# Second-half convolution beside the first half's attention, a norm in other PSUM banks, and softmax scaling on GpSimd

## The chip, the cores and the metric

The kernel runs on one core of a Trainium2 chip. A core has five engines that run their own instruction streams and wait for each other by semaphores: TensorE (PE in the profile: matrix products and transposes; PEld is its weight load), VectorE (DVE), ScalarE (ACT), GpSimd (POOL) and SyncE (SP, which here issues most of the loads). Tiles lie in SBUF, and the results of TensorE in PSUM, which is divided into banks of 128 partitions by 512 fp32 values. The metric is the device time of one execution in microseconds (us).

## The reference

One decoder layer on 1024 tokens of width 1024, in fp32. The parts that this change touches are the token mixer's two groups:

```python
proj = x @ w_in + b_in
q, k, v, a, gate = jnp.split(proj, [Q_END, K_END, V_END, A_END], axis=-1)
# attention group: window 128, 8 heads, 2 kv heads, a sink per head
scores = jnp.where(mask, scores + bias[:, :, None], -jnp.inf)
m = jnp.maximum(jnp.max(scores, axis=-1, keepdims=True), sink)
p = jnp.exp(scores - m)
denom = jnp.sum(p, axis=-1, keepdims=True) + jnp.exp(sink - m)
probs = (p / denom).astype(v.dtype)
# convolution group
h = a * jax.nn.sigmoid(gate)
h = causal_depthwise_conv(h, dw_w, dw_b)      # 31 taps, 512 channels
h = layer_norm(h, ln_g, ln_b)
y_conv = jax.nn.silu(h)
y = jnp.concatenate([rms_norm(y_attn, attn_out_gain), rms_norm(y_conv, conv_out_gain)], axis=-1)
mix = y @ w_out + b_out
```

After it come `x = layer_norm(alpha * x + mix)`, an up-projection to 2 x 2816 channels, a convolution of width 3, a SwiGLU gate, a down-projection and a last layer norm.

## The kernel before

**Tiling.** The 1024 tokens are two halves (H = 0 and 1) of 512 tokens, a half four blocks (`TB`) of 128. Activations lie transposed, channels on partitions and 512 tokens along the free axis, so that a projection product is one PSUM tile of 128 x 512. To get fp32 accuracy every operand is split into a high and a low part (`split_part`: the high part by ScalarE, line 232, the low one by GpSimd, line 234), and `mm3` makes a product of 24 matmuls: 8 of high with high (line 266), 8 of high with low (267), 8 of low with high (269). The feed-forward part runs for most channels on both halves together (`joint`, a seven-product scheme, lines 790 to 793), for the first six channel chunks on each half alone.

**Stages of a half.** `glu(H, c)` makes the 128 channels of convolution group c: two products into two PSUM tiles, a sigmoid on ScalarE, and one VectorE operation (line 356) that writes the convolution's input `hconv`. `proj_kv` and `proj_q` make keys, values and queries. `conv(H)` takes the four groups in two pairs (`conv_pair`): 26 (H = 1) or 27 (H = 0) of the 31 taps of a group are VectorE operations that accumulate in a PSUM tile of the C banks (lines 419 and 423; the last writes SBUF), and the remaining taps are a multiplication on ScalarE (409) and an addition on GpSimd (413); line 428 joins them. `conv_norm(H)` is the layer norm over the 512 channels, done with matmuls against ones: the mean (443), the variance (454), a product that spreads the reciprocal deviation (462), and after the swish the mean square for the RMS norm (478). Each of these four has a PSUM tile; VectorE reads them on lines 447, 290, 467 and 290.

`attn(H)` has 16 units, one for each block, kv group and pair of heads, in a software pipeline of 21 steps. `front` makes scores (TensorE, 509), adds the bias and finds the row's maximum (VectorE, 514), takes the exponential with its sum and that of the sink (ScalarE, 519 and 521). With the second pair of a group come the sum of the denominators (525), their reciprocal (526) and the scaling of four tiles of 128 x 256 (529). `mid` transposes (539) and splits (541, 542), `back` multiplies with the values (560 to 562) and reads out (567, 569, 572); `tail` is the mean square of the attention output (579). `out_proj(H)` is the output projection (640 to 652) on top of the residual rows that it loads and scales first (625); `ln1(H)` the layer norm after it, with transposes (277 to 281).

**What sets the order.** The stages are Python generators, and the string `SCRIPT` says in which order their steps are written down: each letter advances one of them by a step. `0`: a GLU group of half 0, `x`: a block of the second half's input, `j`/`k`: kv, `i`/`q`: a product of q, `c`/`C`: the convolution of half 0/1, `n`/`N`: its norm, `a`/`A`: an attention step, `g`: a GLU group of half 1, `o`/`O`: output projection, `l`/`L`: layer norm, `f`: feed-forward of half 0, `s`: sums for `joint`. `c` and `C` ran a convolution to its end at once. From this program order a scheduler, at compile time, places the instructions into the engines' streams, by priority and by its own estimate of the times; an instruction earlier in the program goes first when both are ready. Three orders are held by hand: big products keep their order (`chain`), taps keep theirs (`tap`), and loads keep theirs on SyncE's queue (`load`).

**PSUM.** Five tags share the eight banks: A, S and C have two each, T and Y one. `PT` says which tag a stage's tiles take in turn. In the mixer, the products of `glu1`, `kv1`, `q0` and `q1` and of both output projections take A; scores take S; transposes and attention tails T; attention outputs Y; convolution chains C, and before the change the norm's four tiles took C as well. A tile waits until a bank of its tag is free.

**SBUF.** Places are given by hand (`LANES`). The second half's residual rows (`acc`) lie where the second half's `hconv` and the second norm's temporaries (`LANES_NORM1`) lie.

Of the kernel before, what the change touches and what calls it, by code (L numbers as in the profile page):

```python
# [12 lines left out]
AF = mybir.ActivationFunctionType  # L13
ALU = mybir.AluOpType

P = 128
S = 1024
D = 1024
# [15 lines left out]
LINE = 384  # L34
GROUP = 2
ALONE = 6
SCRIPT = ('0hx00j0hxixxiiiacaaaaaaaaaaaaannnaaagaggqqgaaaqkqoAAAoAAAAAo'
          'ACAoAAllAANAAAANAlAlfNfAOOOfOffLLLLsffffsss')
SKEW = (1, 2, 5)
KOFF = (4, 5)  # L40
# [2 lines left out]
XM = (1, 1)  # L43
PT = {'x0': 'AT', 'x1': 'AS', 'glu0': 'AS', 'glu1': 'A', 'kv0': 'A', 'kv1': 'A', 'q0': 'A', 'q1': 'A', 'v0': 'T', 'v1': 'T',
      'joint': 'ATSACSYC',
      'tail': 'T', 'out0': 'A', 'out1': 'A', 'ln0': 'A', 'ln1': 'A', 'up0': 'AY', 'up1': 'AY', 'down0': 'SCY', 'down1': 'S'}
PS = {'A': 2, 'S': 2, 'T': 1, 'Y': 1, 'C': 2}
UNIT = 512
BASE = 384
# [21 lines left out]
def hybrid_layer_kernel(  # L71
# [7 lines left out]
    nc = tc.nc  # L79
# [22 lines left out]
    def psB(shape=(P, 512), tag="T"):  # L102
        return ps.tile(list(shape), F32, name="ps" + tag, tag=tag, bufs=PS[tag])
# [3 lines left out]
    def psk(key, shape=(P, 512)):  # L107
        tags = PT[key]
        k = ps_turn[key] = ps_turn.get(key, -1) + 1
        return psB(shape, tags[k % len(tags)])  # L110

    def f(ap):
        return ap.bitcast(F32)
# [58 lines left out]
    sink = small[:, 8:16]  # L172
# [151 lines left out]
    def pair(i):  # L324
        return area(2 * i), area(2 * i + 1)
# [109 lines left out]

    def conv_norm(H):
        y = cyt[H]
        mean = psB(tag="C")
        sums = [sbt([P, HALF], "nsum") for _ in range(2)]
        for i in range(2):  # L440
            nc.gpsimd.tensor_tensor(out=sums[i], in0=y[2 * i], in1=y[2 * i + 1], op=ALU.add)
        nc.gpsimd.tensor_tensor(out=sums[0], in0=sums[0], in1=sums[1], op=ALU.add)
        nc.tensor.matmul(out=mean, lhsT=ones, rhs=sums[0], start=True, stop=True)
        var = psB((P, 4), "C")
        sqs = []
        for c in range(4):
            nc.vector.tensor_tensor(out=y[c], in0=y[c], in1=mean, op=ALU.subtract)
            sq = sbt([P, HALF], "nsq")
            nc.scalar.square(out=sq, in_=y[c])
            sqs.append(sq)  # L450
        yield
        for t in range(TB):
            for c in range(4):
                nc.tensor.matmul(out=var[:, t:t + 1], lhsT=sqs[c][:, t * P:(t + 1) * P], rhs=ones[:, 0:1],
                                 start=c == 0, stop=c == 3)
        rstd = ring("crstd", 4, 2)
        rsqrt_eps(rstd, var, 4, "nrv")
        dg = sbt([P, TB, P], "nz")
        for t in range(TB):
            nc.vector.tensor_scalar(out=dg[:, t, :], in0=ident, scalar1=rstd[:, t:t + 1], scalar2=None, op0=ALU.mult)  # L460
        rb = psB(tag="C")
        nc.tensor.matmul(out=rb, lhsT=ones1, rhs=dg, start=True, stop=True)
        yield
        yh, yl = [[a[:, c, :] for c in range(4)] for a in pair(1)]
        sqs = []
        for c in range(4):
            nc.vector.tensor_tensor(out=y[c], in0=y[c], in1=rb, op=ALU.mult)
            nc.scalar.activation(out=y[c], in_=y[c], func=AF.Silu, bias=clb[c], scale=clg[c])
            nc.scalar.mul(out=yh[c], in_=y[c], mul=gain[4 + c])
            nc.vector.scalar_tensor_tensor(out=yl[c], in0=y[c], scalar=gain[4 + c], in1=f(yh[c]),  # L470
                                           op0=ALU.mult, op1=ALU.subtract)
            sq = sbt([P, HALF], "nsq")
            nc.scalar.square(out=sq, in_=y[c])
            sqs.append(sq)
        ms = psB((P, 4), "C")
        for t in range(TB):
            for c in range(4):
                nc.tensor.matmul(out=ms[:, t:t + 1], lhsT=sqs[c][:, t * P:(t + 1) * P], rhs=ones[:, 0:1],
                                 start=c == 0, stop=c == 3)
        s = ring("sC", 4, 2)  # L480
        rsqrt_eps(s, ms, 4, "nrv")
        yC[H] = (yh, yl)
        sC[H] = s
        yield

    def attn(H):
        bias = bias_t[0]
# [5 lines left out]
        def front(u):  # L493
            t, g, pr = u
            b = H * TB + t
            qh, ql = [a[:, :, t * P:(t + 1) * P] for a in qT[H]]
            gs = slice(g * HD, (g + 1) * HD)
            k0 = max(b - 1, 0) * P
            ks = slice(k0, k0 + 2 * P)
            lo = P if b == 0 else 0  # L500
            nk = 2 * P - lo
            sc = psB((P, 2, 2 * W), "S")
            pt = sbt([P, 2, 2 * W], "p")
            if pr == 0:
                sms[t, g] = ring("sm", 12, 4)
            m, es, den = [sms[t, g][:, 4 * k:4 * k + 4] for k in range(3)]
            for i in range(2):
                for n, (a, c) in enumerate(((qh, kh), (qh, kl), (ql, kh))):
                    nc.tensor.matmul(out=sc[:, i, :], lhsT=a[gs, 2 * pr + i, :], rhs=c[gs, ks],  # L509
                                     start=n == 0, stop=n == 2)  # L510
            h0 = g * 4 + pr * 2
            for i in range(2):
                h, j = h0 + i, 2 * pr + i
                nc.vector.tensor_tensor_reduce(
                    out=pt[:, i, lo:], in0=sc[:, i, 0:nk], in1=bias[h0 // 2][:, i, lo:], op0=ALU.add, op1=ALU.min,
                    scale=1.0, scalar=nsink[:, h:h + 1], accum_out=m[:, j:j + 1])
            for i in range(2):
                h, j = h0 + i, 2 * pr + i
                nc.scalar.activation(out=pt[:, i, lo:], in_=pt[:, i, lo:], func=AF.Exp, bias=m[:, j:j + 1],
                                     scale=-1.0, accum_out=den[:, j:j + 1])  # L520
                nc.scalar.activation(out=es[:, j:j + 1], in_=sink[:, h:h + 1], func=AF.Exp, bias=m[:, j:j + 1],
                                     scale=1.0)
            pts[u] = pt
            if pr == 1:
                nc.vector.tensor_tensor(out=den, in0=den, in1=es, op=ALU.add)
                nc.vector.reciprocal(out=den, in_=den)
                for j in range(4):
                    q = pts[t, g, j // 2][:, j % 2, lo:]
                    nc.scalar.mul(out=q, in_=q, mul=den[:, j:j + 1])

        def mid(u):
            b = H * TB + u[0]
# [385 lines left out]
    def drain(*gens):  # L918
        gens = list(gens)
        while gens:  # L920
            for g in list(gens):
                try:
                    next(g)
                except StopIteration:
                    gens.remove(g)
# [52 lines left out]
    norm1 = []  # L978
# [26 lines left out]
    parameters()  # L1005
    for k in SCRIPT:
        if k in 'cC':
            drain(steps[k])
        else:
            next(steps[k], None)  # L1010
    drain(*steps.values())
# [59 lines left out]
```

## Time and profile before

| | us |
|---|---|
| runs of the kernel | 1151.25, 1154.1, 1156.5 (median 1154.1) |
| the profiled execution | 1154.67 |
| its span, first to last instruction | 1152.9 |
| mean granted clock of TensorE over the span | 0.958 of full |

The times are those of whole executions; the profile is of one execution, whose own time stands beside its span. In the rows below a line such as L423 is a line of the kernel, an arrow points from inputs to the output (out<-in), and a time is counted from the span's start. A row that shows an engine busy tells how long its instructions took, not that each was needed at that moment; idle time of an engine names what ended it.

### The profile page before, as it was taken

The page shows a single profiled execution, that of the slowest core. Times are in us where ns is not written, and L with a number is a line of the kernel's source. Part 1 is how long each engine was busy: PE and PEld are TensorE (multiplying, and loading weights), DVE is VectorE, ACT ScalarE, POOL GpSimd, SP SyncE. Part 2 cuts the span into 40 slices and gives each one's busy share as a digit, 9 for nine tenths or more (in the row PEclk, how much of TensorE's full clock was granted, in tenths as well). Part 3 has the DMA queues.
Part 4 walks back from the last instruction along what each step waited for, and adds up shares of the span by engine and source line. Part 5 has one row for each costly group of instructions (what it writes and reads, how often), then busy time and mean ns, then how long its engine had stood idle before and what let it go on. Part 6 is the DMA issues. An engine that isn't in the chain of part 4 may idle for free.

```text
span 1152.9 us, 14636 instructions
## 1 busy us (share of the span) xinstructions
PE 1085.0 (94%) x5257; PEld 907.7 (79%) x5257; DVE 796.6 (69%) x1406; ACT 521.8 (45%) x1031; POOL 627.5 (54%) x484
## 2 busy tenths in 40 slices
PE   7999999998898999894999999999999999999997
PEld 5877788888787799683778787887878787888875
DVE  2699556999994436889784747465665656559666
ACT  4536897673678322453342425152424242442530
POOL 4739644365451255867856556463637373735561
PEclk9999988999977899997999999999999999999999
DMA  5544213124101333221121212121202021133421
GB/s 177 165 100 120 74 26 98 52 85 144 38 1 54 102 99 94 76 71 37 37 73 37 74 37 74 37 65 32 69 19 89 22 73 37 56 109 110 128 92 73
DMA packets 115643, 85.21 MB, mean 74 GB/s; under 512 B 20355, under 2 KB 108018, under 8 KB 115570
## 3 DMA queue, kind: packets, MB, share of 16 engines
q1 hardware_dynamic: 112368, 78.92, 23.1%
q10 hardware_dynamic: 3201, 5.35, 1.3%
q8 instruction: 41, 0.67, 0.2%
q14 instruction: 33, 0.26, 0.1%
HBM read 80.05 MB, written 4.21 MB: 73 GB/s over the span
## 4 chain that ended last, share of the span: by engine, by line
PE 71%; DVE 18%; DMA 4%; ACT 4%; POOL 1%; issue 1%; SPq 0%; POOLq 0%; DVEq 0%; ACTq 0%
PE psA L266 4%; PE psA L267 4%; PE psA L269 4%; DVE psC L423 4%; DVE cy L745 3%; PE psC L793 2%; PE psS L509 2%; PE psC L790 2%; PE psC L791 2%; PE psS L713 2%; PE psS L714 2%; PE psS L715 2%; PE psS L790 2%; PE psS L791 2%; PE psS L793 2%; PE psA L790 2%
## 5 line engine op out<-in xcount | busy, mean ns | idle before, releaser
L234 POOL TENSOR_TENSOR wl<-raw,wh 128x512 fp32r<-128x512 f32 x196 | 267.3, 1375 | 187.4 <-ACT wh L232 80.8
L232 ACT CAST wh<-raw 128x512 fp32r<-128x512 f32 x196 | 118.9, 618 | 169.2 <-PE psA L267 26.8
L234 POOL TENSOR_TENSOR wl<-ts,wh 128x512 fp32r<-128x512 f32 x64 | 83.0, 1304 | 148.3 <-ACT wh L232 136.0
L423 DVE SCALAR_TENSOR_TENSOR psC<-hconv,const,psC 128x512 f32<-128x512 f32 x196 | 135.9, 745 | 0.0
L266 PE MATMUL psA<-x,wh 128*128 128x512 f32 x288 | 115.8, 402 | 3.1 <-ACT wh L232 2.0
L232 ACT CAST wh<-ts 128x512 fp32r<-128x512 f32 x64 | 39.4, 622 | 173.3 <-PE psC L715 31.0
L267 PE MATMUL psA<-x,wh 128*128 128x512 f32 x288 | 115.7, 402 | 0.0
L269 PE MATMUL psA<-x,wl 128*128 128x512 f32 x288 | 76.4, 400 | 0.0
L266 PEld LDWEIGHTS psA<-x,wh 128*128 128x128 f32 x288 | 55.2, 192 | 15.7 <-ACT wh L232 2.3
L267 PEld LDWEIGHTS psA<-x,wh 128*128 128x128 f32 x288 | 55.4, 192 | 11.9 <-issue 0.7
L269 PEld LDWEIGHTS psA<-x,wl 128*128 128x128 f32 x288 | 54.1, 191 | 12.7 <-issue 1.0
L291 POOL TENSOR_TENSOR tiny<-tiny,const 128x1 f32<-128x1 f32 (+1 forms) x28 | 26.5, 950 | 68.0 <-DVE tiny L290 68.0
L234 POOL TENSOR_TENSOR ol<-or,oh 128x512 fp32r<-128x512 f32 x32 | 40.5, 1292 | 32.5 <-ACT oh L232 32.5
L720 DVE TENSOR_TENSOR acc<-psS,acc 128x512 f32<-128x512 f32 x48 | 32.9, 687 | 24.5 <-PE psS L715 24.4
L790 PE MATMUL psS<-x,wh 128*128 128x512 f32 x112 | 43.7, 390 | 0.8 <-ACT wh L232 0.8
L790 PE MATMUL psA<-x,wh 128*128 128x512 f32 x112 | 44.2, 395 | 0.0
L791 PE MATMUL psA<-x,wh 128*128 128x512 f32 x112 | 44.0, 393 | 0.0
L791 PE MATMUL psS<-x,wh 128*128 128x512 f32 x112 | 43.6, 389 | 0.0
L790 PE MATMUL psC<-x,wh 128*128 128x512 f32 x112 | 43.6, 389 | 0.0
L791 PE MATMUL psC<-x,wh 128*128 128x512 f32 x112 | 43.6, 389 | 0.0
L413 POOL TENSOR_TENSOR cp<-cp,cp 128x512 f32<-128x512 f32 x28 | 36.1, 1289 | 13.3 <-ACT cp L409 13.3
L713 PE MATMUL psC<-wh,gh 128*128 128x512 f32 x80 | 32.5, 407 | 11.3 <-ACT gh L693 8.7
(331 smaller groups left out, 3237.5 us busy)
## 6 DMA issues: line engine op xcount, KB each, us to landing
raw<-in_w_up SPq DMA_DIRECT2D x56, 512.0 KB
raw<-in_w_down SPq DMA_DIRECT2D x28, 512.0 KB
raw<-in_w_in SPq DMA_DIRECT2D x20, 512.0 KB
raw<-in_x SPq DMA_DIRECT2D x8, 512.0 KB
raw<-in_w_in SPq DMA_DIRECT2D x16, 256.0 KB
acc<-in_x SPq DMA_DIRECT2D x8, 512.0 KB
or<-in_w_out SPq DMA_DIRECT2D x64, 64.0 KB
or<-in_w_out SPq DMA_DIRECT2D x8, 512.0 KB
```

Source lines behind the costliest of these rows:

```text
L232: nc.scalar.copy(out=h, in_=part)
L234: nc.gpsimd.tensor_tensor(out=l, in0=part, in1=f(h), op=ALU.subtract)
L266: m.append(nc.tensor.matmul(out=o, lhsT=wh[kt], rhs=xh[kt], start=kt == 0, stop=False))
L267: m.append(nc.tensor.matmul(out=o, lhsT=wh[kt], rhs=xl[kt], start=False, stop=False))
L269: m.append(nc.tensor.matmul(out=o, lhsT=wl[kt], rhs=xh[kt], start=False, stop=kt == KT - 1))
L413: nc.gpsimd.tensor_tensor(out=extra[c], in0=extra[c], in1=prod, op=ALU.add)
L423: tap(nc.vector.scalar_tensor_tensor(out=to, in0=src, scalar=cdw(k, c), in1=chains[c], op0=ALU.mult, op1=ALU.add))
L713: m.append(nc.tensor.matmul(out=o, lhsT=gh[:, tsl], rhs=wh, start=j == 0, stop=False))
L745: nc.vector.tensor_tensor(out=o, in0=o, in1=x_, op=ALU.add if s_ > 0 else ALU.subtract)
L790: m.append(nc.tensor.matmul(out=o, lhsT=wh[k], rhs=xh[k], start=k == 0, stop=False))
L791: m.append(nc.tensor.matmul(out=o, lhsT=wh[k], rhs=xl[k], start=False, stop=False))
L793: m.append(nc.tensor.matmul(out=o, lhsT=wl[k], rhs=xh[k], start=False, stop=k == 3))
```

## The change

Four edits.

- The script. Two `g` steps (the second half's GLU groups 0 and 1) stand ahead of the first attention step `a`, instead of after the first half's norm. A new letter `D` advances the second half's convolution by one step: three D directly after the first half's norm `nnn`, a fourth after the fourth `g`; `C` runs what is left. A step of `conv_pair` ends after the taps 24, 16 and 8 of a pair, so the first three D write the first pair's taps from 30 down to 8, and the fourth its last ones and the second pair's down to 24. One `q` and one `g` change places.
- The norm's PSUM tiles are taken through `psk` under the names `norm0` and `norm1`: the first norm's come from A, the second's from C as before.
- The exponential of the sink: instead of one ScalarE operation per head, VectorE adds the sink and the negated maximum for four heads, and one ScalarE operation takes the exponential of the four.
- The scaling of the probabilities goes from ScalarE to GpSimd, as a `tensor_scalar` with two multiplications (the second by 1).

```diff
-SCRIPT = ('0hx00j0hxixxiiiacaaaaaaaaaaaaannnaaagaggqqgaaaqkqoAAAoAAAAAo'
+SCRIPT = ('0hx00j0hxixxiiiggacaaaaaaaaaaaaannnDDDaaagaqgDqaaaqkqoAAAoAAAAAo'
           'ACAoAAllAANAAAANAlAlfNfAOOOfOffLLLLsffffsss')
...
+      'norm0': 'A', 'norm1': 'C',
...
     def conv_norm(H):
-        mean = psB(tag="C")
+        mean = psk("norm%d" % H)
...
-        var = psB((P, 4), "C")
+        var = psk("norm%d" % H, (P, 4))
...
-        rb = psB(tag="C")
+        rb = psk("norm%d" % H)
...
-        ms = psB((P, 4), "C")
+        ms = psk("norm%d" % H, (P, 4))
...
+            if pr == 1:
+                nc.vector.tensor_tensor(out=es, in0=sink[:, g * 4:g * 4 + 4], in1=m, op=ALU.add)
             for i in range(2):
                 h, j = h0 + i, 2 * pr + i
                 nc.scalar.activation(out=pt[:, i, lo:], in_=pt[:, i, lo:], func=AF.Exp, bias=m[:, j:j + 1],
                                      scale=-1.0, accum_out=den[:, j:j + 1])
-                nc.scalar.activation(out=es[:, j:j + 1], in_=sink[:, h:h + 1], func=AF.Exp, bias=m[:, j:j + 1],
-                                     scale=1.0)
             pts[u] = pt
             if pr == 1:
+                nc.scalar.activation(out=es, in_=es, func=AF.Exp)
                 nc.vector.tensor_tensor(out=den, in0=den, in1=es, op=ALU.add)
                 nc.vector.reciprocal(out=den, in_=den)
                 for j in range(4):
                     q = pts[t, g, j // 2][:, j % 2, lo:]
-                    nc.scalar.mul(out=q, in_=q, mul=den[:, j:j + 1])
+                    nc.gpsimd.tensor_scalar(out=q, in0=q, scalar1=den[:, j:j + 1], scalar2=1.0,
+                                            op0=ALU.mult, op1=ALU.mult)
...
     for k in SCRIPT:
         if k in 'cC':
             drain(steps[k])
+        elif k == 'D':
+            next(steps['C'])
         else:
             next(steps[k], None)
```

More of the change, by code (lines that the diff above doesn't have):

```diff
@@ L45 @@
       'joint': 'ATSACSYC',
-      'tail': 'T', 'out0': 'A', 'out1': 'A', 'ln0': 'A', 'ln1': 'A', 'up0': 'AY', 'up1': 'AY', 'down0': 'SCY', 'down1': 'S'}
+      'norm0': 'A', 'norm1': 'C', 'tail': 'T', 'out0': 'A', 'out1': 'A', 'ln0': 'A', 'ln1': 'A', 'up0': 'AY', 'up1': 'AY', 'down0': 'SCY', 'down1': 'S'}
 PS = {'A': 2, 'S': 2, 'T': 1, 'Y': 1, 'C': 2}
```

## The prediction

> **What bounds the kernel now.** I read the page first, then busy time in stretches, then the chain of waits, and last the rows of single lines. Of the page, the busy line and the chain by engine:
>
> ```profile
> PE 1085.0 (94%) x5257; PEld 907.7 (79%) x5257; DVE 796.6 (69%) x1406; ACT 521.8 (45%) x1031; POOL 627.5 (54%) x484
> ...
> PE 71%; DVE 18%; DMA 4%; ACT 4%; POOL 1%; issue 1%; SPq 0%; POOLq 0%; DVEq 0%; ACTq 0%
> ```
>
> TensorE bounds most of the span, and no product is taken away. So only stretches in which TensorE is not well fed can be shortened; the chain puts 18% on VectorE. The change touches the work between 104 us and 400 us: both attentions, the second half's GLU and convolution, the two convolution norms. Busy time by stretch there:
>
> ```profile
> core 0: us, PE busy (x) PEld busy (x) DVE busy (x) ACT busy (x) POOL busy (x), PEclk, DMA share, GB/s
> ...
> 128.00:192.00 64.00, 64.00 (x322) 52.41 (x321) 32.05 (x82) 57.44 (x130) 35.91 (x32) 0.90 0.19 49
> 192.00:232.00 40.00, 40.00 (x209) 33.19 (x207) 38.12 (x68) 23.72 (x57) 16.27 (x12) 0.99 0.28 91
> 232.00:250.00 18.00, 17.55 (x130) 15.95 (x130) 18.00 (x43) 11.73 (x37) 9.03 (x8) 1.00 0.42 122
> 250.00:276.00 26.00, 22.09 (x156) 20.87 (x157) 25.93 (x55) 14.14 (x33) 20.60 (x19) 0.91 0.14 42
> ...
> 290.00:324.00 34.00, 30.56 (x205) 27.49 (x205) 33.35 (x82) 20.50 (x67) 18.09 (x14) 0.90 0.10 32
> 324.00:346.00 22.00, 20.36 (x107) 18.39 (x107) 20.42 (x43) 17.00 (x39) 10.29 (x7) 0.69 0.00 1
> 346.00:370.00 24.00, 18.82 (x95) 17.61 (x94) 11.74 (x31) 23.20 (x51) 3.11 (x3) 0.72 0.02 2
> 370.00:381.00 11.00, 8.14 (x42) 7.82 (x41) 7.09 (x10) 3.24 (x6) 1.53 (x2) 0.66 0.80 260
> ```
>
> Columns are busy us with instruction counts, then TensorE's granted clock. Read them as three stages. From 128 to 232 TensorE is full and VectorE is half idle at first (32.05 of 64 us). From 232 to 324 VectorE is full: 18.00 of 18, 25.93 of 26, 33.35 of 34. From 324 to 381 nothing is full but ScalarE (23.20 of 24), and the clock is near 0.7: work waits for work there. What fills VectorE from 192 on are the taps of the second half's convolution, line 423 alone in the stretches 104 to 128, 128 to 192, 192 to 232 and 232 to 313:
>
> ```profile
> 104.00:128.00 24.00, 17.09 (x25) 1.00 0.27 69
> 128.00:192.00 64.00, 0.87 (x2) 0.90 0.19 49
> 192.00:232.00 40.00, 23.61 (x34) 0.99 0.28 91
> 232.00:313.00 81.00, 46.73 (x65) 0.94 0.32 93
> ```
>
> So there are no taps in the very stretch in which VectorE is idle. The timeline of VectorE and the chain of waits (PE rows) tell why:
>
> ```profile
> 143.71 0.86 PE psC L443 x2
> 150.51 0.56 PE psC L454 x6
> 164.71 0.86 PE psC L462 x2
> 176.51 0.54 PE psC L478 x4
> ...
> 144.60 2.48 DVE L447 TENSOR_TENSOR cy<-cy,psC 128x512 f32<-128x512 f32 x4 [1.85 <-PE psC L443]
> 157.25 0.15 DVE L290 TENSOR_SCALAR tiny<-psC 128x4 f32<-128x4 f32 x1
> 165.61 2.48 DVE L467 TENSOR_TENSOR cy<-cy,psC 128x512 f32<-128x512 f32 x4 [0.39 <-PE psC L462]
> 173.44 0.81 DVE L419 TENSOR_SCALAR psC<-hconv,const 128x512 f32<-128x512 f32 x1
> 188.82 0.16 DVE L290 TENSOR_SCALAR tiny<-psC 128x4 f32<-128x4 f32 x1 [0.46 <-PE psC L478]
> 190.38 0.81 DVE L419 TENSOR_SCALAR psC<-hconv,const 128x512 f32<-128x512 f32 x1
> ```
>
> The first norm's four PSUM tiles (mean, variance, spread, mean square) and the two tap chains share the two C banks. The first chain opens (L419) at 173.44 after the spread was read, the second at 190.38 after the mean square was. The taps start some 45 to 60 us after the first convolution is through.
>
> What ends late because of them:
>
> ```profile
> SPq L132 <- PE psC L478: 56.5, 2, 56.0
> ...
> 370.41 7.67 DMA acc<-in_x
> ```
>
> The load queue stands 56.0 us until the second norm's last product (L478) has released the storage that the second half's residual rows go into; those land until 378, and the loads of w_out for the second half are queued behind them. So the end of the taps, then the second norm, then these loads pace the start of the second output projection. After 400 us nothing is touched, and I carry the shift through unchanged.
>
> **The change, part by part.** The sum is against the profiled execution's own 1154.67 us (span 1152.9 and 1.8 around it), 0.6 above the median of 1154.1.
>
> (a) *Norm 0 out of the C banks, and three D steps before the last attention units.* They free VectorE's idle time for the first pair's 52 taps (2 openings, 50 of line 423). One costs 46.73/65 = 0.72 us. The idle time from 128 to 192 is 64 - 32.05 = 32 us, room for 44 taps. The rest of the pair follows by about 200. The second pair waits for its last input:
>
> ```profile
> L356 DVE SCALAR_TENSOR_TENSOR hconv<-psA,const,z x8: 716/744/751, 28.6 to 203.2; 128x512 f32<-128x512 f32 x8
> ```
>
> From 203 to 232, taps at the present share of VectorE (23.61/40 = 0.59) come to 29 x 0.59/0.72 = 24. So 76 of 104 are done by 232, where now some 37 are: 39 fewer remain, 39 x 0.72 = **28 us** off the full stage. Ends: 14 us if only half of the idle time can be used (its gaps are short, 1.85 us ahead of L447, and a tap in one delays the next attention step), 47 us if no tap is left after 232. I take 28, since taps in 192 to 232 got 0.59 beside the same attention work. The multiplications and additions on ScalarE and GpSimd for the first pair (L409, L413) already run early and stay.
>
> (b) *Norm 0 into the A banks.* This adds a wait. From the rows above a norm tile is held 143.7 to 147.1, 150.5 to 157.4, 164.7 to 168.1 and 176.5 to 189.0: 26.2 us in all. All products of glu(1), kv and q go through the same two A banks.
>
> ```profile
> 199.59 1.82 PE psA L269 x8
> ...
> L397 ACT ACTIVATE z<-psA,const 128x512 f32<-128x512 f32 x8 | 5.4, 680 | 0.9 <-PE psA L269 0.9
> ```
>
> A product of 24 matmuls takes 24 x 1.82/8 = 5.5 us and its read-out 0.68. With one bank left, read-out no longer hides: 26.2/6.2 = 4.2 products x 0.7 = 3 us. A GLU wants both banks at once, so its second product also waits for half of a short hold, another 3. Queued behind a waiting product on TensorE are the later products (their order is fixed by hand); attention matmuls can fill in. These 6 us also put off the second pair's input: 6 x 0.59/0.72 = 5 taps, 4 us less of (a). I take 6 + 4 = **+10**; ends 0 (all filled) and, if bulk work stands for every hold, 26 and 26 x 0.59 = 15, together +41.
>
> (c) *ScalarE gives up work.*
>
> ```profile
> L529 ACT ACTIVATE hank<-hank,tiny 128x256 f32<-128x256 f32 x56 | 24.1, 501 | 4.0 <-DVE tiny L526 4.0
> L521 ACT ACTIVATE tiny<-const,tiny 128x1 f32<-128x1 f32 x64 | 18.1, 282 | 0.0
> L529 ACT ACTIVATE hank<-hank,tiny 128x128 f32<-128x128 f32 x8 | 2.5, 388 | 0.0
> ...
> 324.00:370.00 46.00, 5.19 (x12) 0.71 0.01 2
> ...
> L379 POOL MEMSET vpad<- 128x512 f32 x8 | 3.8, 526 | 0.3 <-POOLq L1050 0.3
> L234 POOL TENSOR_TENSOR ol<-or,oh 128x512 fp32r<-128x512 f32 x32 | 40.5, 1292 | 32.5 <-ACT oh L232 32.5
> ...
> L525 DVE TENSOR_TENSOR tiny<-tiny x16: 145/295/1209, 118.1 to 362.5; 128x4 f32<-128x4 f32 x16
> ```
>
> The scalings (24.1 + 2.5) and 48 of the 64 sink exponentials (48 x 0.282 = 13.5) go: 40 us off ScalarE. Most lies beside a full TensorE (128 to 232) or VectorE (232 to 324), and is worth nothing there. From 324 to 370 ScalarE has 40.2 of 46 us; the fourth row is line 529 in that stretch: 12 scalings of 5.19 us go, and of the exponentials beside them about as many, with 8 x 0.28 = 2 us. Of these 7 some two thirds lie on the chain: **-5**, ends 0 and -10. The 16 new additions on VectorE (some 0.15 to 0.3 us) are 4 us spread over 250, and go into the ends.
>
> (d) *Scaling on GpSimd.* The trace has no scaling there. Bounds for 128x256: half of the MEMSET, 0.26 us, and a whole two-input operation, 1.29. I take half of that, 0.65, the nearest arithmetic. 64 x 0.65 = 42 us find room: in the stretches listed GpSimd is busy 115 of 239 us. But a group of four lies between reciprocal and transposes: 4 x 0.65 = 2.6 against 4 x 0.5 = 2.0. In the first half TensorE's other work covers it; of the second half's eight groups none is covered once VectorE is no longer full: 8 x 0.6 = **+5**. Ends 0, and +15 if each also waits for a weight split ahead of it in the queue (1.29). Splits queued behind a scaling are prefetches. [...]
>
> (e) *Two GLU groups earlier in the script.* Their 4 loads, casts, splits and 96 matmuls keep their place after q's fourth product in the load queue and in the chain of products; they only go ahead of the first attention units, which are also TensorE work. **0**, ends 0 and +4.
>
> Sum: -28 + 10 - 5 + 5 = -18. 1154.67 - 18 = 1136.7; against the median **1136**. Its own range is 1120 to 1146.
>
> [...]
>
> **The rivals.**
> 1. *Full relief.* No tap is left after 232, and 324 to 381 closes up: (a) gives 47, (b) costs its 6 alone, (c) and (d) cancel: 1154 - 41, about 1113. For: VectorE is the only full engine there. Against: the second pair cannot begin before 203.
> 2. *The next wait is close behind.* Attention of the second half ends the stage too:
>
> ```profile
> L567 ACT ACTIVATE x<-psY,const x32: 345/368/390, 155.0 to 384.1; 128x128 fp32r<-128x128 f32 x32
> ```
>
> Its last read-out starts at 384.1, after the 378 of the loads. If its units are slow for their own latency, only the taps beside its last units go:
>
> ```profile
> 290.00:324.00 34.00, 10.87 (x15) 0.90 0.10 32
> ```
>
> That is 11 us, and with (b) at 6 and (c) and (d) cancelling, 5 remain: 1149. For: 60 us of attention still follow the last taps, though VectorE is not full there. Against: the second norm, late for the taps, runs in the same queues.
> 3. *The script doesn't decide.* A scheduler places every instruction at compile time. If taps land where they were, about 1154. Against: the bank is what held them, and it is freed.
> 4. *Slower: A banks.* If bulk products stand for all 26 us of the holds, the last input of the second pair comes at about 229 and (a) shrinks to 28 - 15 = 13: +26 - 13 = +13, about 1167. Each us that bulk work stands costs 1 + 0.59, so this outweighs (a) from 28/1.59 = 18 of the 26 us. For: glu(1)'s third and fourth groups fall into the holds. Against is the count of line 266, 8 of a product's 24 matmuls, from 128 to 192:
>
> ```profile
> 128.00:192.00 64.00, 19.54 (x46) 9.18 (x45) 0.90 0.19 49
> ```
>
> That is 46 x 3 = 138 bulk matmuls of 322; the others can fill a hold.
>
> **How the numbers follow.** Forecast 0.50, rival 1 0.15, rival 2 0.13, rival 3 0.08, rival 4 0.14. 0.5% (about 6 us) is what a measurement of this kernel can tell from no change: faster is below 1148. Faster: 0.50 + 0.15 + half of rival 2 = 0.71. Slower is rival 4, 0.14; the same, 0.15, is rival 3 and the rest of 2. The range leaves out rival 4 and the outer parts of rivals 1 and 3: 1106 to 1155.
>
> **What would show it.** Right: line 419 opens near 131 and line 423 runs through 131 to 200; the last tap ends by about 285; the acc loads land by about 350; granted clock from 320 on above 0.85. Wrong: L266 rows waiting for norm reads (L447, L467, L290) between 140 and 190 say rival 4; taps over by 285 but the acc loads or the last L567 still past 370 say rival 2. A GpSimd scaling above 1 us breaks (d). A span after the second output projection that grows breaks the shift that I carry through.

## The result, and the profile after

The changed kernel takes 1160.85 us (median of 8 runs, 1158.18 to 1164.15) where the kernel before takes 1154.08 (8 runs). The ratio is put at 1.0065, with a 95% interval of 1.0045 to 1.0085 (the two medians alone make 1.0059): **slower by 0.65%**, where 1136 was forecast. The profiled execution has a span of 1156.4 us against 1152.9. Three of the ten executions of g_only below, the profiled one among them, were disturbed, so its row leaves them out and has no trace. The changed kernel has two more lines from line 515 on, so L526, L529 and L567 of before are now L527, L530 and L569.

The page after, busy line and chain by engine:

```profile
PE 1084.7 (94%) x5257; PEld 907.0 (78%) x5257; DVE 796.1 (69%) x1422; ACT 486.0 (42%) x917; POOL 656.1 (57%) x548
...
PE 70%; DVE 19%; ACT 4%; DMA 4%; POOL 1%; issue 1%; SPq 0%; POOLq 0%; DVEq 0%; ACTq 0%
```

ScalarE gave up 35.8 us and GpSimd took 28.6; the chain is shared out as before. The difference lies in the stretches. Busy time by stretch, after:

```profile
128.00:192.00 64.00, 56.16 (x232) 44.90 (x230) 58.93 (x137) 38.77 (x91) 29.77 (x38) 0.65 0.07 17
...
290.00:324.00 34.00, 34.00 (x272) 32.32 (x270) 20.32 (x57) 18.48 (x47) 19.35 (x23) 1.00 0.47 132
324.00:346.00 22.00, 21.72 (x176) 20.51 (x174) 20.37 (x57) 9.65 (x28) 11.93 (x10) 1.00 0.01 2
346.00:370.00 24.00, 17.08 (x89) 15.22 (x90) 17.75 (x43) 21.20 (x43) 11.47 (x16) 0.79 0.10 33
```

From 128 to 192 VectorE went from 32.05 to 58.93 us, as it was to. But TensorE went from 322 matmuls at a clock of 0.90 to 232 at 0.65. It makes up for them later: from 290 to 324, where VectorE was the full engine (33.35 of 34), TensorE is now full and VectorE has 20.32. The relief of one engine became a backlog of the other.

The rows of the lines that mark the ends of the work (instructions, their shortest, median and longest duration in ns, first and last start in us), before:

```profile
L423 DVE SCALAR_TENSOR_TENSOR cy<-hconv,const,psC x6: 730/735/740, 125.5 to 311.9; 128x512 f32<-128x512 f32 x6
...
L562 PE MATMUL psY<-ph,vpad x16: 280/415/420, 341.9 to 381.0; 128*128 128x256 f32 x16
...
L266 PE MATMUL psY<-x,wh x16: 387/396/628, 381.2 to 397.5; 128*128 128x512 f32 x16
```

and after:

```profile
L423 DVE SCALAR_TENSOR_TENSOR cy<-hconv,const,psC x6: 718/738/742, 122.7 to 277.9; 128x512 f32<-128x512 f32 x6
...
L356 DVE SCALAR_TENSOR_TENSOR hconv<-psA,const,z x4: 748/750/751, 116.4 to 220.4; 128x512 f32<-128x512 f32 x4
...
L478 PE MATMUL psC<-const,nsq x32: 211/251/373, 356.5 to 366.8; 128*128 128x1 f32 x32
...
L564 PE MATMUL psY<-ph,vpad x14: 278/283/416, 342.4 to 386.2; 128*128 128x256 f32 x14
...
L266 PE MATMUL psY<-x,wh x16: 388/392/487, 386.4 to 401.4; 128*128 128x512 f32 x16
```

Read the last start in each row. The last tap (L423) starts 34.0 us earlier, at 277.9. The last attention product with the values (before L562, after L564) starts 5.2 us **later**, at 386.2. The last row is the feed-forward's second product, the first that takes the bank Y, in which attention's outputs lie: it starts as the last value product is through, 381.2 before and 386.4 after, again 5.2 later. The rest of the span from there is 1152.9 - 381.2 = 771.7 before and 1156.4 - 386.4 = 770.0 after. So in these two traces attention's end is what reaches the time, not the taps'.

Why TensorE stood back from 128 on: the high-with-high matmuls of the bulk products (L266 alone) by stretch, after,

```profile
128.00:169.00 41.00, 0.00 (x0) 0.00 (x0) 0.62 0.05 14
169.00:192.00 23.00, 8.11 (x16) 4.24 (x16) 0.71 0.11 24
192.00:236.00 44.00, 18.38 (x47) 8.94 (x48) 1.00 0.36 109
236.00:252.00 16.00, 6.71 (x18) 3.09 (x17) 1.00 0.02 4
```

and VectorE's reads of the first norm's tiles in its timeline, after:

```profile
142.66 2.45 DVE L447 TENSOR_TENSOR cy<-cy,psA 128x512 f32<-128x512 f32 x4
...
155.33 0.15 DVE L290 TENSOR_SCALAR tiny<-psA 128x4 f32<-128x4 f32 x1
...
164.49 2.48 DVE L467 TENSOR_TENSOR cy<-cy,psA 128x512 f32<-128x512 f32 x4
```

For 41 us no bulk product runs, though the norm starts to write its last tile (the mean square) only at 168.8. The next product begins at 169.2, after the spread was read (164.49 + 2.48 = 166.97); the one behind it at 185.9, after the mean square was read at 182.7. The mean's bank was free from 145 and the variance's from 155.5, but went to the spread and the mean square, which stand ahead of the third GLU group in the program and were not yet computed. Here a **bank is handed out in the order of the program**, not to whoever is ready.

The hole could also be a wait for weights. It isn't: the high parts of the weights (L232) and the low ones (L234), two of each per product, from the span's start to 135 us after, and the next low part behind the hole:

```profile
L232 ACT CAST wh<-raw x42: 603/618/627, 13.8 to 126.6; 128x512 fp32r<-128x512 f32 x42
...
L234 POOL TENSOR_TENSOR wl<-raw,wh x41: 1270/1293/1324, 14.5 to 130.2; 128x512 fp32r<-128x512 f32 x41
...
175.46 1.29 POOL L234 TENSOR_TENSOR wl<-raw,wh 128x512 fp32r<-128x512 f32 x1 [12.46 <-PE psA L269]
```

Eighteen products had run when the hole began, and the weights of twenty were split by 131.5, both products of the third GLU group among them. The next split then waits for a product, so that the loads stand still too: that follows from the hole and doesn't cause it.

### The profile page after: what moved, and what is told of

Same layout as the page of the kernel before. It is cut to its first block, busy times and chain, and to the rows that moved or that the text cites. A ratio compares the mean times of both kernels' runs of the same rounds, so it can differ in the third digit from the quotient of the medians.

```text
span 1156.4 us, 14665 instructions
## 1 busy us (share of the span) xinstructions
PE 1084.7 (94%) x5257; PEld 907.0 (78%) x5257; DVE 796.1 (69%) x1422; ACT 486.0 (42%) x917; POOL 656.1 (57%) x548
## 4 chain that ended last, share of the span: by engine, by line
PE 70%; DVE 19%; ACT 4%; DMA 4%; POOL 1%; issue 1%; SPq 0%; POOLq 0%; DVEq 0%; ACTq 0%
DVE psC L423 5%; PE psA L266 3%; PE psA L267 3%; PE psA L269 3%; DVE cy L747 3%; PE psC L793 2%; PE psC L792 2%; PE psS L715 2%; PE psS L792 2%; PE psS L793 2%; PE psS L795 2%; PE psC L795 2%; PE psS L716 2%; PE psS L717 2%; PE psA L795 2%; PE psA L793 2%
## 5 line engine op out<-in xcount | busy, mean ns | idle before, releaser
L234 POOL TENSOR_TENSOR wl<-raw,wh 128x512 fp32r<-128x512 f32 x196 | 268.2, 1380 | 149.8 <-ACT wh L232 58.6
L232 ACT CAST wh<-raw 128x512 fp32r<-128x512 f32 x196 | 118.9, 619 | 177.1 <-PE psA L267 34.5
L234 POOL TENSOR_TENSOR wl<-ts,wh 128x512 fp32r<-128x512 f32 x64 | 82.9, 1304 | 148.5 <-ACT wh L232 135.6
L423 DVE SCALAR_TENSOR_TENSOR psC<-hconv,const,psC 128x512 f32<-128x512 f32 x196 | 134.2, 745 | 0.0
L266 PE MATMUL psA<-x,wh 128*128 128x512 f32 x288 | 117.0, 406 | 3.0 <-ACT wh L232 2.0
L232 ACT CAST wh<-ts 128x512 fp32r<-128x512 f32 x64 | 39.3, 622 | 172.9 <-PE psS L717 30.9
L266 PEld LDWEIGHTS psA<-x,wh 128*128 128x128 f32 x288 | 56.3, 196 | 15.5 <-ACT wh L232 2.3
L234 POOL TENSOR_TENSOR ol<-or,oh 128x512 fp32r<-128x512 f32 x32 | 40.6, 1292 | 35.1 <-ACT oh L232 28.3
L530 POOL TENSOR_SCALAR hank<-hank,tiny 128x256 f32<-128x256 f32 (+1 forms) x64 | 30.6, 499 | 25.0 <-DVE tiny L527 9.9
```

The source lines that it names most:

```text
L232: nc.scalar.copy(out=h, in_=part)
L234: nc.gpsimd.tensor_tensor(out=l, in0=part, in1=f(h), op=ALU.subtract)
L266: m.append(nc.tensor.matmul(out=o, lhsT=wh[kt], rhs=xh[kt], start=kt == 0, stop=False))
L423: tap(nc.vector.scalar_tensor_tensor(out=to, in0=src, scalar=cdw(k, c), in1=chains[c], op0=ALU.mult, op1=ALU.add))
```

## Experiments

Three theories at first. A: the norm in the A banks holds the bulk products back (above). B: the scaling on GpSimd costs the time. C: the early taps do, in VectorE's queue. Later P, that the second norm's end sets the time, and W, that the last attention units of the second half do. All 15 kernels (g_only and g_again are one), each with its ratio to the kernel before run beside it, and with last starts from their traces as in the rows above (tap is L423, norm is L478, value is L564 or its counterpart, feed is the first feed-forward product in the Y bank):

| kernel | median us | ratio to before, 95% | tap | norm | value | feed |
|---|---|---|---|---|---|---|
| before | 1154 | 1 | 311.9 | 369.1 | 381.0 | 381.2 |
| changed | 1160.9 | 1.0065 (1.0045 to 1.0085) | 277.9 | 366.8 | 386.2 | 386.4 |
| n_only | 1166.0 | 1.0094 (1.0065 to 1.0123) | 298.6 | 376.5 | 394.8 | 394.9 |
| s_g | 1167.2 | 1.0101 (1.0085 to 1.0117) | 314.5 | 378.3 | 384.4 | 391.8 |
| s_n | 1164.1 | 1.0072 (1.0050 to 1.0094) | 283.7 | 382.8 | 392.3 | 392.5 |
| g_only | 1158.0 | 1.0007 (0.9978 to 1.0035) | | | | |
| g_again | 1158.1 | 1.0045 (1.0026 to 1.0063) | 321.4 | 380.0 | 374.6 | 380.2 |
| s_only | 1161.7 | 1.0067 (1.0045 to 1.0088) | 296.0 | 368.6 | 386.9 | 387.1 |
| n_spread | 1143.4 | 0.9913 (0.9886 to 0.9939) | 251.9 | 347.5 | 375.8 | 375.9 |
| n_t | 1174.1 | 1.0173 (1.0139 to 1.0207) | 232.8 | 292.3 | 398.3 | 398.4 |
| late_early | 1166.2 | 1.0122 (1.0077 to 1.0166) | 277.9 | 365.7 | 388.3 | 391.8 |
| spread_early | 1148.6 | 0.9950 (0.9931 to 0.9969) | 250.9 | 346.8 | 376.9 | 377.1 |
| spread_s | 1150.2 | 0.9966 (0.9950 to 0.9983) | 250.3 | 347.5 | 379.8 | 380.0 |
| spread_4 | 1150.2 | 0.9960 (0.9940 to 0.9980) | 253.3 | 340.1 | 379.0 | 379.1 |
| o_late1 | 1147.6 | 0.9946 (0.9928 to 0.9963) | 252.1 | 348.3 | 372.0 | 377.6 |
| o_late2 | 1145.7 | 0.9931 (0.9904 to 0.9959) | 253.4 | 338.7 | 369.7 | 375.3 |

**The parts, one and two at a time.** n_only is the kernel before with the first norm in A:

```diff
-        mean = psB(tag="C")
+        mean = psk("norm%d" % H)
...
+      'norm0': 'A', 'norm1': 'C',
```

> Only the first norm's four tiles move to the A banks; script and scaling stay as before. Theory A (the two banks of a tag are handed out in program order, so whatever asks for A behind the norm waits until its third and fourth tiles have been read, here the second half's first GLU group): a hole of 40 us or more without bulk products (lines 266, 267, 269) between 104 and 170 us, and a time of 1165 to 1200. Theory B (GpSimd scaling holds up the attention and the weight splits): scaling is not changed here, so no hole, and 1151 to 1157. Theory C (the D taps on VectorE hold up attention): no taps moved, so 1151 to 1157.

s_g is the changed kernel with the norm back in the C banks:

```diff
-      'norm0': 'A', 'norm1': 'C',
+      'norm0': 'C', 'norm1': 'C',
```

> The changed kernel with the first norm's tiles back in the C banks; new script and GpSimd scaling stay. Theory A: bulk products go on without the hole from 128 to 169, the first tap chain of the second half opens only after the norm's third tile is read (170 to 195 us) as before, and the time is 1147 to 1156. Theory B: the hole stays and the time stays at 1158 to 1163. Theory C: the taps cannot start early, so the time also falls to 1150 to 1157, but then without any change in what bulk products wait for.

s_n is the changed kernel with the scaling and the sink's exponentials as before:

```diff
+                nc.scalar.activation(out=es[:, j:j + 1], in_=sink[:, h:h + 1], func=AF.Exp, bias=m[:, j:j + 1],
+                                     scale=1.0)
...
-                    nc.gpsimd.tensor_scalar(out=q, in0=q, scalar1=den[:, j:j + 1], scalar2=1.0,
-                                            op0=ALU.mult, op1=ALU.mult)
+                    nc.scalar.mul(out=q, in_=q, mul=den[:, j:j + 1])
```

> The changed kernel with exponential and scaling back on ScalarE; new script and first norm in A stay. Theory A: the hole of some 40 us without bulk products stays and the time is 1157 to 1172. Theory B: the hole goes and the time falls to 1150 or less.

g_only has these two edits alone, and nothing else of the change; g_again is the same kernel once more, and the one whose trace is read.

> The kernel before with only the exponential and scaling edits. Theory A: these cost little or win a little, 1148 to 1156. Theory B: they cost what the whole change costs, 1158 to 1163.

> The exponential and scaling edits alone, for a trace of them. No change in time (0.998 to 1.004 of before). L530 near 0.5 us. Theory: ScalarE's 40 us of relief lie beside TensorE and VectorE, so the last tap still ends within 5 us of 313, and the second norm's last product (L478) within 5 us of 369.

s_only has the script alone:

```diff
-SCRIPT = ('0hx00j0hxixxiiiacaaaaaaaaaaaaannnaaagaggqqgaaaqkqoAAAoAAAAAo'
+SCRIPT = ('0hx00j0hxixxiiiggacaaaaaaaaaaaaannnDDDaaagaqgDqaaaqkqoAAAoAAAAAo'
```

> The script edit alone: first norm in the C banks, scaling on ScalarE. Theory A says that without the norm in A there is no hole in the bulk products, and that taps wait for the C banks as in the kernel before: no change, 1149 to 1160. If the two GLU groups ahead of the attention cost something by themselves, it shows here: 1160 to 1170, as with the script edit and the GpSimd scaling together (1167).

n_only has the hole too (the bulk products pause from 104.9 to 160.2) and costs 0.9%, as A expected. Without the scaling on GpSimd (s_n) the loss stays: B falls. Without the norm in A (s_g) the hole is gone, but the taps wait for the C banks as before (L419 opens at 171.3), and the time is worse still: A's number for it, 1147 to 1156, missed, and so did C's, 1150 to 1157. C falls with n_spread below, which keeps the early taps and is the fastest of all. So each of the script and the norm's move costs by itself (0.67% and 0.94%), and they don't add up when put together. For s_only the dearer of the two expected cases came. The scaling and exponential edits alone cost nothing to half a per cent. In g_again the last value product starts 6.4 us earlier than before, but the last tap 9.5 and the second norm's last product 10.9 us later, so the expected ends of both were missed, as was the ratio (1.0045, where at most 1.004 was expected):

```profile
L564 PE MATMUL psY<-ph,vpad x12: 278/282/415, 340.6 to 374.6; 128*128 128x256 f32 x12
...
L478 PE MATMUL psC<-const,nsq x32: 206/352/373, 368.2 to 380.0; 128*128 128x1 f32 x32
```

There the gain was handed from one end of the stage to another. In s_g the feed-forward starts 7.4 us behind the last value product; the waits of TensorE in s_g, from 355 to 400, name ScalarE's last read of attention's output (line 574):

```profile
PE psY L266 <- ACT sq L574: 7.0, 1, 7.0
```

**Is it the order of the banks?** n_spread keeps the whole change and only writes the first norm's second and third steps behind the third and fourth GLU group:

```diff
-SCRIPT = ('0hx00j0hxixxiiiggacaaaaaaaaaaaaannnDDDaaagaqgDqaaaqkqoAAAoAAAAAo'
+SCRIPT = ('0hx00j0hxixxiiiggacaaaaaaaaaaaaanDDDaaagnaqgDnqaaaqkqoAAAoAAAAAo'
```

> The changed kernel with the first norm's three steps spread in the script among the GLU, tap and attention steps, instead of all three before the third GLU group. Theory A (bank order: a product stands behind the norm's tiles because banks of a tag are handed out in program order): the third GLU group's products now come between the norm's tiles, so the 41 us hole in the bulk products (128 to 169) falls to under 15 us, the last q product of the second half ends near 232 instead of 252, and the span falls by most of the 23 us of backlog: 1130 to 1148. Theory P (the time follows the end of the second norm, which waits for the first output projection, and not the backlog): the hole goes, but the time falls only as far as the second norm's mean-square product (L478, 367 in the changed kernel) comes earlier: 1150 to 1160 if that stays within 5 us.

The bulk matmuls of line 266 by stretch in n_spread, and then its last tap, last value product and first product in Y:

```profile
128.00:169.00 41.00, 7.28 (x16) 3.30 (x16) 0.79 0.17 39
169.00:192.00 23.00, 9.27 (x23) 4.36 (x24) 0.92 0.16 47
192.00:236.00 44.00, 16.77 (x42) 8.06 (x41) 0.96 0.23 74
236.00:252.00 16.00, 0.00 (x0) 0.00 (x0) 0.79 0.37 96
```

```profile
L423 DVE SCALAR_TENSOR_TENSOR cy<-hconv,const,psC x6: 714/736/742, 123.4 to 251.9; 128x512 f32<-128x512 f32 x6
...
L478 PE MATMUL psC<-const,nsq x32: 352/352/373, 336.9 to 347.5; 128*128 128x1 f32 x32
...
L564 PE MATMUL psY<-ph,vpad x12: 278/284/416, 355.8 to 375.8; 128*128 128x256 f32 x12
...
L266 PE MATMUL psY<-x,wh x16: 387/389/486, 375.9 to 390.9; 128*128 128x512 f32 x16
```

Two products now run between the norm's tiles (16 matmuls of line 266 from 128 to 169, none in the changed kernel), and all bulk work is through by 236 instead of 251.4. The ratio goes from 1.0065 to 0.9913: with no operation changed, the order alone is worth 1.5%, some 17 us, and the kernel is **faster than both**. In the two traces the span falls by 10.2 us, and the last value product's start by 10.4; the profiled executions took 1158.2 and 1148.0, while the medians are 17.5 apart. A's claim that the order of the banks makes the hole holds, and its time and its end of the last q product (235.7, where 232 was expected) came. Its number for the hole didn't: instead of under 15 us, two stretches without bulk products are left, of 11 us (129.0 to 140.3) and of 18 (154.5 to 172.7). Of P's number, 1150 to 1160 unless L478 came over 5 us earlier, no more can be said here: it came 19 us earlier, and the time 17 less.

n_t puts the first norm into the single T bank ('norm0': 'T'), which the attention's transposes use.

> The changed kernel with the first norm's tiles taken from the T banks (attention transposes) instead of A. Theory A: no hole in the bulk products, taps open near 125 to 132 as in the changed kernel and end by 285; the first half's attention stands behind the norm's tiles instead, for up to 26 us of holds, beside bulk work that fills TensorE: 1130 to 1150. Theory P: as for the other kernel, 1150 to 1160 if L478 ends later than 360.

```profile
L564 PE MATMUL psY<-ph,vpad x24: 277/281/415, 343.1 to 398.3; 128*128 128x256 f32 x24
...
L478 PE MATMUL psT<-const,nsq x32: 352/352/373, 246.4 to 262.7; 128*128 128x1 f32 x32
L478 PE MATMUL psC<-const,nsq x32: 165/250/353, 283.2 to 292.3; 128*128 128x1 f32 x32
...
L423 DVE SCALAR_TENSOR_TENSOR cy<-hconv,const,psC x6: 716/736/745, 122.0 to 232.8; 128x512 f32<-128x512 f32 x6
```

A's places came (no hole, the taps over by 285), but its time, 1130 to 1150, missed, and P's does not apply, as L478 ended long before 360. This run tells most. The taps end 79 us earlier than before, the second norm 77 us earlier (292.3 against 369.1), and the kernel is the slowest of all, since attention ends at 398.3. P falls as the one rule: with the norm's end 77 us earlier, the time is longer.

**The second norm's place.** late_early writes the second norm's steps earlier; spread_early does both edits.

```diff
-          'ACAoAAllAANAAAANAlAlfNfAOOOfOffLLLLsffffsss')
+          'ACNAoANAllAANAAAAAlAlffAOOOfOffLLLLsffffsss')
```

> The changed kernel with the second norm's steps written earlier in the second part of the script (first step two letters after the taps, the second four letters later, the third right behind the last output projection step). The hole from 128 to 169 stays. Theory A (the hole's backlog of 23 us on TensorE is what took the gain): no change against the changed kernel, 1155 to 1165. Theory P (the second norm's queueing behind the first output projection's products took it): L454 ends before 320 instead of 341, L478 ends 10 us earlier or more, and the time falls to 1142 to 1152.

> Both script edits together. If A alone holds: as with the spread first norm alone, 1130 to 1148. If P alone holds: as with the earlier second norm alone, 1142 to 1152. If each takes a part of the gain: lower than either, 1125 to 1140.

Writing the steps earlier moved L478 by 1.1 us in the changed kernel and by 0.7 in n_spread, and both read slower, by some 0.4 to 0.6%, with intervals that overlap those of the kernels without it. So the place in the script was not what held the second norm, and P could not be tested by it; that late_early keeps its loss and spread_early its gain speaks for A.

**What is left of the hole, and the scaling beside it.** spread_s is n_spread with the exponentials and the scaling on ScalarE. spread_4 divides the norm's second step, so that a product stands between variance and spread:

```diff
+        if H == 0:
+            yield
         rb = psk("norm%d" % H)
...
-SCRIPT = ('0hx00j0hxixxiiiggacaaaaaaaaaaaaanDDDaaagnaqgDnqaaaqkqoAAAoAAAAAo'
+SCRIPT = ('0hx00j0hxixxiiiggacaaaaaaaaaaaaanDDDaaagnaqnagDnqaaaqkqoAAAoAAAAAo'
```

> The kernel with the norm's steps spread, with the scaling and the sink's exponentials back on ScalarE. If the GpSimd scaling (64 of 0.5 us) costs the weight splits behind it their place, this is faster than with it: 1133 to 1141. If ScalarE's relief is worth the 5 us that the prediction gave it, slower: 1146 to 1152. If neither, 1141 to 1147.

> The kernel with the norm's steps spread, and its second step divided in two (variance, then spread), so that a bulk product stands between each two of the norm's tiles: script n after the convolution, n after the third GLU group, n after the q product behind it, n after the fourth tap step. Theory A: the 18 us without bulk products that are left (154 to 173) shrink to under 8, the last q product ends 6 to 10 us earlier than 236, and the time is 1132 to 1142. If the rest of that hole is something else (the weights, the attention's own matmuls), no change: 1142 to 1147.

spread_s is 0.5% behind n_spread, the case expected for a ScalarE whose relief counts: here it is worth some 6 us. In spread_4 the stretch without bulk products from 154 to 173 shrank to 9 us (154.9 to 163.8), but another of 11 opened from 191.5 to 202.4, the last q product came no earlier (238.3 against 235.7), and the time rose to 1150.2, outside both of its expected ranges: the rest of the hole isn't worth what its first part was, or this order pays for it elsewhere; that isn't settled.

**Why only 10 of 60 us arrive.** o_late1 and o_late2 take n_spread and write one or all steps of the first output projection later among the second half's attention steps:

```diff
-          'ACAoAAllAANAAAANAlAlfNfAOOOfOffLLLLsffffsss')
+          'ACAAAoANAAllAAANAlAlfNfAOOOfOffLLLLsffffsss')
```

> The kernel with the first norm's steps spread, and the last step of the first output projection written two attention steps later (the two transposing steps of the layer norm behind it move along). Theory W (the time is the end of the second half's last attention value product plus 767 us of untouched work, and that attention shares TensorE with the first output projection until 324 us): the last value product ends before 372 instead of 376, the second feed-forward product starts with it, and the span falls by as much: 1136 to 1142. If the attention's end is set by its own latency or by ScalarE and VectorE from 324 on, it stays at 374 to 380: 1142 to 1150. In either case the span minus the end of the last value product is 765 to 771.

> As the other, with all four steps of the first output projection one to four attention steps later. Theory W: as the other or better, last value product before 370, 1133 to 1142. If the layer norm and the feed-forward weights behind the projection become late in its place, the second feed-forward product starts over 3 us behind the last value product, and the time is 1145 to 1158.

The last value product moved about as W says, from 375.8 to 372.0 and 369.7, so that attention does end late because it shares TensorE with the projection. The time did not follow: o_late1 took 1147.6 (not 1136 to 1142), and o_late2 1145.7, the case expected for a layer norm that comes late (1145 to 1158; its second feed-forward product starts 5.6 us behind the last value product). From the last value product's start to the span's end it was 770.4 us in n_spread, and is now 774.8 and 776.0, so the expected 765 to 771 was missed too. The feed-forward's first and second products and the last value product in o_late1:

```profile
L564 PE MATMUL psY<-ph,vpad x12: 282/415/416, 349.6 to 372.0; 128*128 128x256 f32 x12
...
L266 PE MATMUL psA<-x,wh x16: 389/389/393, 372.1 to 386.2; 128*128 128x512 f32 x16
L266 PE MATMUL psY<-x,wh x16: 387/389/486, 377.6 to 392.6; 128*128 128x512 f32 x16
```

In n_spread the first of the two ran before the attention's end (356.3); now it starts at 372.1, and the second one product later, at 377.6. The chain that ended last tells whom the first waits for, in o_late1:

```profile
360.29 0.92 POOL hank L530 x2
...
362.94 2.38 POOL acc L310
365.34 1.24 DVE acc L311
366.62 1.13 PE psA L277 x4
```

The layer norm of the first half stands on GpSimd (L310) behind the scalings of the attention (L530), and its transposes (L277) feed the product. So a third chain, output projection, layer norm, feed-forward, lies close to the attention's end: in o_late1 its first product starts only as the attention ends, and the second stands 5.5 us behind it.

## Why the prediction was wrong

**(a) Taps into VectorE's idle time: right as a relief, wrong as time.** 28 us off the end of the taps were forecast, 34.0 came, and L419 opened at 124.0. But the sum carried these 28 us to the end one for one: this step failed. The runs show that they don't arrive: in n_spread the last tap starts 60.0 us earlier and the second norm's last product 21.6, while the last value product starts 5.2 us earlier, the span of the same trace is 6.7 us shorter, and the time by the ratio some 10 us less. This is the mechanism of rival 2, attention's own end right behind, and the profile before had it in view: acc landed at 378 and the last value product started at 381.0. Its signs came in the changed kernel: the taps are over by 279, but the acc loads land at 376.7 and the last read-out of attention (L569) starts at 388.2. The acc loads were to land by 350.

**(b) The norm in the A banks: the step that turned the sign.** It said "With one bank left, read-out no longer hides: 26.2/6.2 = 4.2 products x 0.7 = 3 us" and took +10, with 41 as its outer end. This is the other step that failed. It counted only the time in which a tile was held, and let the other bank serve the products. In its place the runs show 41 us without any bulk product, since a bank that falls free goes to the norm's next tile in the program. The last input of the convolution came at 220.4 instead of 203.2, the first output projection's last matmul at 333.9 instead of 309.7, the last value product 5.2 us later. Breaking the hole in two by order alone, with all bulk work through some 15 us earlier, was worth 17 us and gave the forecast sign back. The +10 itself is near what n_only measures, 0.94% or some 11 us. That is luck: the pause there is 55 us long, where the sum had 6 us of waits and 4 of lost taps. And it can't simply be added to the rest: s_g, which is the changed kernel with the norm back in C, takes longer (1.0101) than the changed kernel (1.0065), and its taps wait again.

**Rival 4** had the place and the sign, and 1167. Its route was another: the bulk products stood for 41 us and not 26, and the taps, which it gave 13 us, came 34 us earlier. The price went through TensorE's backlog into the second half's attention, which o_late1 and o_late2 bear out: less projection beside it, and its last value product comes earlier (372.0 and 369.7 against 375.8). Its sign, "L266 rows waiting for norm reads (L447, L467, L290)", did not show as such rows: L266 is missing altogether from 128 to 169.

**(c) and (d): near zero together, as summed, but not fixed.** The larger shape of the scaling in the profile after:

```profile
L530 POOL TENSOR_SCALAR hank<-hank,tiny 128x256 f32<-128x256 f32 x56 | 27.7, 515 | 24.1 <-DVE tiny L527 9.0 <-PE psS L509 4.6 <-ACT x L469 3.7
```

It takes 0.515 us in the mean, where 0.65 was taken, and ScalarE took 0.501 for the same shape before: the groups of four became hardly longer, so the +5 for them was too much. Both edits together measured 0.07% and 0.45% slower alone, 0.34% slower on top of the script (s_g against s_only), 0.07% faster in the changed kernel (against s_n) and 0.53% faster in n_spread (against spread_s). Only the last, and the 0.45%, are clear of their intervals. That the worth of an engine's relief depends on which chain ends last fits these numbers, but no run shows it.

**(e) Two GLU groups earlier, costed at 0.** The script alone, which includes the four D steps with their taps waiting for the C banks, costs 0.67%, some 8 us, where 0 to 4 was allowed. From 232 to 290, first in the kernel before and then in s_only:

```profile
232.00:290.00 58.00, 52.34 (x380) 48.93 (x380) 54.91 (x121) 30.89 (x82) 34.60 (x30) 0.94 0.38 111
...
232.00:290.00 58.00, 45.30 (x319) 42.28 (x318) 55.33 (x122) 30.05 (x84) 28.53 (x25) 0.88 0.29 88
```

TensorE does only 45.30 of 58 us of work there, 7 us less than before, beside a VectorE that is nearly full in both, and the last value product starts 5.9 us later than before, although the last bulk product is 5 us earlier. Which step of the script does it wasn't tried, and stays open.

**Rival 3** falls: the taps moved where the script put them. **The shift carried through** after 400 us holds: from the first product in the Y bank to the end of the span it is 768 to 774 us in all 15 traces. The clock above 0.85 from 320 on came only to 346: it was 1.00 there, with TensorE busy for 25.72 of 26 us by its backlog, and 0.79 from 346 to 370, with 17.08 of 24.

## What to carry to other kernels

Before a tile moves to another pool of banks, write down who stands behind it there in the program: a bank is lost from the moment that its turn comes, not from the first write (here no bulk product ran from 128 to 169, and the mean square was first written at 168.8), so small tiles of a long dependent chain belong between the large ones and not ahead of them. Relief of a full engine counts only as far as the next chain that ends the stage lets it (here 60.0 us at the taps' end in n_spread, and some 10 in the time); list the last start of each of them (here taps, norm, attention, layer norm) before a gain is carried to the end. Where the order is a script, moving the same steps apart can be worth more than the change itself: here 1.5%.

## What was unexpected

In the hole TensorE's granted clock fell to 0.50, with no pause on record above 1.13 us. Busy time by stretch, after, with the granted clock third from the end:

```profile
140.00:150.00 10.00, 7.48 (x28) 5.96 (x28) 10.00 (x22) 6.11 (x13) 7.53 (x12) 0.50 0.01 2
150.00:160.00 10.00, 8.88 (x34) 7.45 (x35) 9.02 (x26) 4.34 (x15) 3.00 (x3) 0.50 0.00 0
```

and the time that single matmuls of line 266 hold TensorE in the chain of the changed kernel, out of the hole:

```profile
170.44 0.43 PE psA L266
...
171.29 0.43 PE psA L266
...
172.60 0.24 PE psA L266
```

From 140 to 160 the clock is at half, though TensorE is idle for 2.52 us in all in the first ten and 1.12 in the second; its longest idle time on record from 128 to 160 is 1.13 us (a matmul's end in the records is modelled). The first matmuls behind the hole hold the engine 1.8 times as long (0.43 against 0.24). In the kernel before, the clock was 0.69 to 0.72 from 324 to 370, where the longest idle time on record is 2.83 us. By what rule the clock falls, no run shows. In the changed kernel it was 0.50 beside attention's few short matmuls, 28 to 34 in 10 us; over all of 128 to 169 it was 0.92 in the kernel before, with 30 matmuls of line 266, 0.79 in n_spread with 16, and 0.62 in the changed kernel with none. So here the hole in the bulk work was paid twice, as missing products and as slow ones.
